# Two inner tiles of a feed-forward stage fed step by step at the start of a kernel, with a fixed order on TensorE and the inputs loaded first

## The chip, the cores and the metric

The kernel runs on one core of one Trainium2 chip. The metric is the device time of one execution, in microseconds. A profiled execution also has a span, from its first to its last instruction, which is a little shorter than its time.

## The reference

A two-layer backbone over 256 latent tokens x and 256 context tokens y, all of width 1024. Around each layer's token mixer (differential attention in layer 0, Fourier mixing in layer 1) stand two SwiGLU feed-forward stages, each behind an RMS norm and a shift and scale that are made from a condition vector:

```
m = silu(cond) @ w_mod + b_mod                    # per layer: 9 rows of 1024 (shift, scale, gate, three times)
h = rms_norm(x, norm_g) * (1 + scale) + shift
g, u = split(h @ w_gu)                            # D_FF = 2816
x = x + 0.5 * gate * ((silu(g) * u) @ w_d)
```

All is fp32, and the result must have fp32 accuracy. Latent tokens use the condition c, context tokens c_ctx. The change concerns only the start of the first of these stages in layer 0, on all 512 tokens.

## The kernel before, in words

The width of 1024 lies in 8 tiles of d with 128 rows each. xy holds both streams as d rows by 512 tokens. Accuracy comes from splitting each operand into a rounded part (hi) and the rest (lo); a product is then three matmuls, hi*hi, lo*hi, hi*lo (`mm3`, L140 to L143). `split` makes hi on ScalarE (L101) and lo on VectorE (L102), for weights in four pieces (`unit`, L130).

The start (L404 to L447) goes through the words of the table `START` (L31). A digit is `first_products` (L175): load a 1 MB chunk of w_mod (`raw_m`) and multiply it with the silu of both conditions, giving a row of shift and scale for one tile of d (`psr`, then `mrow` by a ScalarE copy). `x0` to `x3` load the inputs, two tiles of d each. `n` sums the squares, then `rstd_cols` (L248) adds them over the rows with products of one column (`ss`), GpSimd takes the power -1/2, four products against the identity spread it over all partitions (`rb`), and ScalarE copies it (`rstd`); VectorE and GpSimd then multiply x by it (`xr`, L443). `f` is `finish`: products of two columns turn the row of one tile of d into columns (`pst`, `first_columns`, L191), VectorE adds the constants (`amul`, `mod`), and shift and scale are applied to `xr` and split into `xop_hi` and `xop_lo`. `g0` and `g1` load and split the weights of the first two inner tiles; `c` loads the two conditions as rows over all partitions (`cond_x`, `cond_y`) and takes their silu (L205).

Then `gate_up` (L304) works through the 22 inner tiles of 128, all 512 tokens wide: for the gate part and the up part, the 8 tiles of d one after the other, 48 matmuls of 128x512 in all (`gu`), then silu on ScalarE (`sg`), a multiplication on VectorE (`hh`) and the split of h. The accumulators `psA` have two buffers, one inner tile each. Beside it VectorE makes the other shifts, scales and gates (`ada_steps`, L210): products of a w_mod chunk with a condition row (`junk`, L201).

All weight loads are issued by SyncE's queue in one order. A scheduler puts each engine's instructions in order by the costs that it assumes and by priorities (`high_priority`, with offsets 60 and 200); on the engines the order is then fixed. Weight tiles rotate in rings (`Ring`, L105), which have more buffers in some stages (`more_buffers`).

Of the kernel before, what the change touches and what calls it, by code (L numbers as in the profile page):

```python
# [14 lines left out]
P = 128  # L15
D = 1024
KT = D // P
NT = 256
# [57 lines left out]
def tile_kernel(ctx: ExitStack, tc, xyT, small, rows, tables, w_mod0, w_mod, w_gu, w_d0, w_d, w_qkv, w_o, w_f, out):  # L76
# [42 lines left out]
    @contextmanager  # L119
    def more_buffers(name, **counts):  # L120
        with ExitStack() as st:
            for tag, n in counts.items():
                pool = st.enter_context(tc.tile_pool(name=f"{name}_{tag}", bufs=n))
                rings[tag].extra = [pool] * n
                rings[tag].i = 0
            yield
            for tag in counts:
                rings[tag].extra = []

    def unit(ap, cols, name):  # L130
        with tc.high_priority(offset=AHEAD):
            raw = rings["raw"].tile(name)
            nc.sync.dma_start(raw[:, :cols], ap)
            hi, lo = rings["whi"].tile(name), rings["wlo"].tile(name)
            for i in range(PIECES):
                c = slice(i * cols // PIECES, (i + 1) * cols // PIECES)
                split(hi[:, c], lo[:, c], raw[:, c])
        return hi, lo

    def mm3(ps, sh, sl, mh, ml, start, stop):  # L140
        PE.matmul(ps, sh, mh, start=start, stop=False)  # L141
        PE.matmul(ps, sh, ml, start=False, stop=False)  # L142
        PE.matmul(ps, sl, mh, start=False, stop=stop)  # L143

    mhalf = const.tile([P, 8], F32, name="mhalf")
    V.memset(mhalf, -0.5)
# [28 lines left out]
    def first_products(dt, spool):  # L175

        raw = rings["raw"].tile(f"m0{dt}")
        nc.sync.dma_start(raw, w_mod0[dt])
        ps = pC(f"psr{dt}")

        for k in range(KT):
            q = k % 4 * 32
            PE.matmul(ps[q:q + 32, :256], cs[:, k, :], raw[:, k * 256:(k + 1) * 256], start=k < 4, stop=k >= 4)
# [7 lines left out]
    def first_columns(dt, row):  # L191
        pt = pB(f"pst{dt}")
        for m in (1, 0):
            PE.matmul(pt[:, 2 * m:2 * m + 2], row[:, m * P:(m + 1) * P], sel, start=True, stop=True)
        V.tensor_scalar(amul[:, 0, :, 0, dt], pt[:, 2:4], bm1[:, dt:dt + 1], sm[:, C_NG + dt:C_NG + dt + 1],
                        op0=ALU.add, op1=ALU.mult)
        V.tensor_scalar_add(mod[:, 0, :, 0, dt], pt[:, 0:2], sm[:, C_BM + dt:C_BM + dt + 1])
# [47 lines left out]
        else:  # L245
            eng.tensor_add(acc[:, sl], acc[:, sl], sq[:, sl])

    def rstd_cols(acc, sl, name):  # L248

        nt = (sl.stop - sl.start) // P  # L250
        ps = pB(f"ss_{name}")
        sq = tails.pop(sl.start)
        for t in range(nt):
            c = slice(sl.start + t * P, sl.start + (t + 1) * P)
            PE.matmul(ps[:, t:t + 1], acc[:, c], ones[:, 0:1], start=True, stop=False)
            PE.matmul(ps[:, t:t + 1], sq[:, c], ones[:, 0:1], start=False, stop=True)
# [6 lines left out]
    def finish_rstd(acc, sl, name, r=None):  # L263
        n = sl.stop - sl.start
        with tc.high_priority(offset=URGENT):
            rc = rstd_cols(acc, sl, name)
            ps = pB(f"rb_{name}")
            for t in range(n // P):
                PE.matmul(ps[:, t * P:(t + 1) * P], rc[:, t:t + 1].to_broadcast([P, P]), ident, start=True, stop=True)
            if r is None:  # L270
                r = work.tile([P, NT], F32, tag="rstd", name=f"rstd_{name}", bufs=2)
            S.copy(r, ps[:, :n])
        return r

    def new_acc(name):
# [7 lines left out]
    def modulated(layer, w, s, r, dt):  # L283
        sl = (SX, SY)[s]
        h = work.tile([P, 512], F32, tag="hh", name="hmod")
        sh = mod[:, layer, s, 3 * w, dt:dt + 1]
        V.scalar_tensor_tensor(h[:, :NT], xy[:, dt, sl], amul[:, layer, s, w, dt:dt + 1], r, op0=ALU.mult, op1=ALU.mult)
        S.activation(xop_hi[:, dt, sl], h[:, :NT], AF.Identity, bias=sh)
        V.scalar_tensor_tensor(xop_lo[:, dt, sl], h[:, :NT], sh, xop_hi[:, dt, sl].bitcast(F32),  # L289
                               op0=ALU.add, op1=ALU.subtract)  # L290


    def scaled_shift(layer, w):
# [7 lines left out]
                               op0=ALU.mult, op1=ALU.subtract)  # L301


    def gate_up(layer, f, j, n, rstd, h_hi, h_lo, jj, fpool):  # L304
        nn = n if rstd is None else NT + 2
        hi, lo = (layer == f == 0 and early.pop(j, None)) or unit(w_gu[layer, f, j], 2048, f"gu{layer}{f}{j}")
        ps = pA(f"gu_{layer}_{f}_{j}")
        for part in range(2):
            for k in range(KT):
                c = k * 256 + part * P  # L310
                mm3(ps[:, part, :nn], hi[:, c:c + P], lo[:, c:c + P], xop_hi[:, k, :nn], xop_lo[:, k, :nn],
                    k == 0, k == KT - 1)
# [12 lines left out]
        split(h_hi[:, jj, :], h_lo[:, jj, :], h[:, :n])  # L325
# [78 lines left out]


    acc = new_acc("l0f0")
    early = {}
    apool = tc.tile_pool(name="ada0", bufs=1)
    apool_ = apool.__enter__()
    conds = [cond_x, apool_.tile([P, D], F32, name="cond_y")]  # L410
    with tc.tile_pool(name="start", bufs=1) as spool, more_buffers("x0", **MORE0):
        def finish(dt):
            with tc.high_priority(offset=URGENT):
                first_columns(dt, begun[dt])
                h = work.tile([P, 512], F32, tag="hh", name="hmod")
                for s, sl in enumerate((SX, SY)):
                    a, sh = amul[:, 0, s, 0, dt:dt + 1], mod[:, 0, s, 0, dt:dt + 1]
                    if s == 0:
                        S.activation(h[:, sl], xr[:, dt, sl], AF.Identity, scale=a, bias=sh)
                    else:  # L420
                        V.tensor_scalar(h[:, sl], xr[:, dt, sl], a, sh, op0=ALU.mult, op1=ALU.add)
                split(xop_hi[:, dt], xop_lo[:, dt], h)

        xr = spool.tile([P, KT, 2 * NT], F32, name="xr")
        rstd0 = spool.tile([P, 2 * NT], F32, name="rstd0")

        pw = pA("warm")
        for _ in range(WARM):
            PE.matmul(pw[:, 0, :P], ones, ones, start=True, stop=True)
        begun = {}  # L430
        for what in START.split():
            if what == "c":
                for s in range(2):
                    condition(conds[s], s)
            elif what[0] == "x":
                i = 2 * int(what[1:])
                nc.sync.dma_start(xy[:, i:i + 2], xyT[:, i:i + 2])
            elif what == "n":
                for i in range(KT):
                    sumsq(acc, i, slice(0, 2 * NT), V)  # L440
                finish_rstd(acc, slice(0, 2 * NT), "l0f0", rstd0)
                for i in range(KT):
                    (V, G)[i in XR_G].tensor_mul(xr[:, i], xy[:, i], rstd0)  # L443
            elif what[0] == "g":
                early[int(what[1:])] = unit(w_gu[0, 0, int(what[1:])], 2048, f"gu00{what[1:]}")
            elif what[0] == "f":
                finish(int(what[1:]))  # L447
            else:
# [472 lines left out]
```

## Time and profile before

| | us |
|---|---|
| median of 3 runs | 1248.56 (1247.15 to 1249.66) |
| the profiled execution | 1248.28 |
| its span | 1246.5 |
| TensorE's products busy | 1219.0 (98%), 8540 instructions |
| TensorE's weight loads busy | 1124.2 (90%) |
| VectorE, ScalarE, GpSimd busy | 906.4, 553.8, 101.9 |

A matmul of full fp32 operands shows as two instructions in the trace and one in the listing of the order; a matmul on split operands is one in both. In the timeline a row is a run of equal instructions: its start, the time from its start to its end, the engine, line and tile, and in brackets the idle time ahead of it with what ended it. Matmuls overlap, so the distance between starts tells more than one's duration. PEclk is TensorE's granted clock: 1.00 is 2.4 GHz, 0.50 is 1.2 GHz.

### The profile page before, as it was taken

To read this page: it belongs to the slowest core of one execution; us is meant where nothing else is said; L and a number is where in the kernel's file an instruction comes from. 1 tells how busy PE (TensorE), PEld (TensorE's weight loads), DVE (VectorE), ACT (ScalarE), POOL (GpSimd) and SP (SyncE) were. 2 spreads that over 40 slices of the span, in tenths; PEclk is the share of its full clock that TensorE was granted. 3 is DMA by queue.
4 is the path that set the end of the run, shared out by engine and by line. 5 is a ranking of instruction groups with operands and counts; after the bars stand their busy time and mean duration, and the time that the engine had idled before them with its cause. 6 is when DMAs were issued, how large, how long until landed. Compare 5 with 4: busy or idle time off the path is not lost. (4 is left out here: it accounts for less than half of the span.)

```text
span 1246.5 us, 21265 instructions
## 1 busy us (share of the span) xinstructions
PE 1219.0 (98%) x8540; PEld 1124.2 (90%) x8540; DVE 906.4 (73%) x1756; ACT 553.8 (44%) x1215; POOL 101.9 (8%) x90
## 2 busy tenths in 40 slices
PE   6899999999999999999999999999999999999998
PEld 4688888888788989998899999999999999999998
DVE  2697985659883777787788787888688767666664
ACT  3432232223133445445545455555455545544552
POOL 1100000000001352340110000110000011000000
PEclk6799999999999899999999999999999999999999
DMA  9555474648881222121465676676686554536532
GB/s 367 212 210 195 171 253 147 215 147 315 302 349 52 84 102 102 61 77 67 156 224 203 246 300 224 210 293 235 206 307 243 176 195 181 181 126 246 188 117 81
DMA packets 37811, 241.94 MB, mean 194 GB/s; under 512 B 4224, under 2 KB 5376, under 8 KB 14672
## 3 DMA queue, kind: packets, MB, share of 16 engines
q1 hardware_dynamic: 37584, 240.25, 52.8%
q8 instruction: 67, 1.10, 0.3%
q0 software_dynamic: 128, 0.33, 0.2%
q14 instruction: 32, 0.26, 0.1%
HBM read 239.51 MB, written 1.05 MB: 193 GB/s over the span
## 5 line engine op out<-in xcount | busy, mean ns | idle before, releaser
L142 PE MATMUL gu<-xop_lo,whi_gu 128*128 128x258 f32 (+1 forms) x1408 | 441.2, 314 | 2.0 <-DVE xop_lo L300 1.5
L141 PE MATMUL gu<-xop_hi,whi_gu 128*128 128x258 f32 (+1 forms) x1408 | 440.7, 314 | 1.7 <-ACT whi_gu L101 1.4
L143 PE MATMUL gu<-xop_hi,wlo_gu 128*128 128x258 f32 (+1 forms) x1408 | 440.1, 313 | 0.1
L101 ACT CAST whi_gu<-raw_gu 128x512 fp32r<-128x512 f32 x352 | 194.8, 618 | 207.1 <-PE gu L142 120.8
L142 PEld LDWEIGHTS gu<-xop_lo,whi_gu 128*128 128x128 f32 x1408 | 268.5, 191 | 19.2 <-DVE xop_lo L300 2.0
L141 PEld LDWEIGHTS gu<-xop_hi,whi_gu 128*128 128x128 f32 x1408 | 268.7, 191 | 18.9 <-ACT whi_gu L101 1.7
L143 PEld LDWEIGHTS gu<-xop_hi,wlo_gu 128*128 128x128 f32 x1408 | 268.8, 191 | 16.7 <-DVE wlo_gu L102 0.4
L102 DVE TENSOR_TENSOR wlo_gu<-raw_gu,whi_gu 128x512 fp32r<-128x512 f32 x352 | 226.8, 691 | 64.6 <-ACT whi_gu L101 63.9
L142 PE MATMUL dn<-h_lo,whi_d 128*128 128x256 f32 (+1 forms) x724 | 219.6, 304 | 0.0
L143 PE MATMUL dn<-h_hi,wlo_d 128*128 128x256 f32 (+1 forms) x724 | 219.5, 304 | 0.0
L141 PE MATMUL dn<-h_hi,whi_d 128*128 128x256 f32 (+1 forms) x724 | 217.7, 304 | 0.4 <-DVE xy L339 0.4
L201 DVE SCALAR_TENSOR_TENSOR junk<-raw_m,cond_x 128x1024 f32<-128x1024 f32 x128 | 156.9, 1226 | 34.7 <-DMA raw_m<-in_w_mod 33.7
L101 ACT CAST whi_d<-raw_d 128x352 fp32r<-128x352 f32 (+2 forms) x256 | 105.9, 484 | 168.9 <-PE gu L142 87.8
L102 DVE TENSOR_TENSOR wlo_d<-raw_d,whi_d 128x352 fp32r<-128x352 f32 (+2 forms) x256 | 121.0, 526 | 54.9 <-ACT whi_d L101 54.9
L141 PEld LDWEIGHTS dn<-h_hi,whi_d 128*128 128x128 f32 x724 | 136.4, 189 | 7.0 <-PE dn L143 0.8
L142 PEld LDWEIGHTS dn<-h_lo,whi_d 128*128 128x128 f32 x724 | 136.8, 189 | 6.2
L143 PEld LDWEIGHTS dn<-h_hi,wlo_d 128*128 128x128 f32 x724 | 136.8, 189 | 6.0
L339 DVE SCALAR_TENSOR_TENSOR xy<-dn,mod,xy 128x256 f32<-128x256 f32 x112 | 50.5, 480 | 58.9 <-PE dn L143 58.7
L510 PE MATMUL pj<-whi_qkv,xop_hi 128*128 128x256 f32 x320 | 92.5, 289 | 0.7 <-DVE kr L556 0.7
L511 PE MATMUL pj<-wlo_qkv,xop_hi 128*128 128x256 f32 x320 | 91.7, 287 | 0.9 <-DVE wlo_qkv L102 0.9
L512 PE MATMUL pj<-whi_qkv,xop_lo 128*128 128x256 f32 x320 | 92.0, 289 | 0.2 <-DVE xop_lo L289 0.2
L101 ACT CAST h_hi<-hh 128x256 fp32r<-128x256 f32 (+1 forms) x88 | 40.3, 460 | 89.0 <-DVE hh L324 60.3
(224 smaller groups left out, 1406.4 us busy)
## 6 DMA issues: line engine op xcount, KB each, us to landing
raw_gu<-in_w_gu SPq DMA_DIRECT2D x88, 1024.0 KB, 5.1
raw_m<-in_w_mod SPq DMA_DIRECT2D x72, 1024.0 KB, 5.8
raw_d<-in_w_d SPq DMA_DIRECT2D x48, 704.0 KB, 4.1
raw_qkv<-in_w_qkv SPq DMA_DIRECT2D x12, 1024.0 KB, 4.8
raw_d<-in_w_d SPq DMA_DIRECT2D x8, 768.0 KB, 4.2
raw_d<-in_w_d SPq DMA_DIRECT2D x8, 640.0 KB, 4.8
raw_wo<-in_w_o SPq DMA_DIRECT2D x4, 1024.0 KB, 4.8
raw_wf<-in_w_f SPq DMA_DIRECT2D x4, 1024.0 KB, 7.2
```

Of the source, the lines that this page charges most:

```text
L101: S.copy(hi, src)
L102: V.tensor_sub(lo, src, hi.bitcast(F32))
L141: PE.matmul(ps, sh, mh, start=start, stop=False)
L142: PE.matmul(ps, sh, ml, start=False, stop=False)
L143: PE.matmul(ps, sl, mh, start=False, stop=stop)
L201: V.scalar_tensor_tensor(junk, w, 1.0, c, op0=ALU.mult, op1=ALU.mult, accum_out=out_col)
L339: V.scalar_tensor_tensor(xy[:, dt, so], ps[:, so.start - sl.start:so.stop - sl.start], mod[:, layer, s, 6 * f + 2, dt:dt + 1], xy[:, dt, s ...
L510: PE.matmul(ps[:, i], xh, wh, start=k == 0, stop=False)
L511: PE.matmul(ps[:, i], xh, wl, start=False, stop=False)
L512: PE.matmul(ps[:, i], xl, wh, start=False, stop=k == KT - 1)
```

## The change

The start is written as one longer table of words, and the products that it names are kept on TensorE in the order of the program (`keep`, a call that holds back the scheduler). The words: `x` loads two tiles of d of the inputs, `l` a chunk of w_mod, `G` and `H` the weights of the first and second inner tile; `p` multiplies a chunk of w_mod, `s` is squares and their sums, `r` spreads rstd, `t` makes the columns of one tile of d, `m` applies norm, shift and scale to one tile of d for both streams (`modulated`, the function that the attention stage already used), `g` and `h` split one piece of the first and second weight tile, behind the last ScalarE instruction of `r` or `m`. `a` and `b` are the six matmuls of one tile of d for the first and second inner tile, in two accumulators at once. `w` is three products of 128x256 whose result nobody reads. `c` loads the condition rows, now behind a one-column copy on GpSimd that reads the last tile's `amul`. `xr` and its multiplications are gone, the warming products are 20 and not 12, and the rings begin a stage with its added buffers.

```diff
-START = "0 x0 1 x1 2 x2 3 x3 n 4 g0 f0 5 f1 f2 6 f3 f4 7 g1 f5 c f6 f7"
-WARM = 12
+START = ("x0 x1 x2 x3 l0 l1 G l2 H l3 l4 l5 p0 s w p1 l6 l7 t0 w t1 w r g0 m0 m1 w g1 a0 p2 a1 h0 t2 m2 b0 p3 b1 h1 t3 m3 "
+         "a2 p4 b2 g2 t4 m4 a3 p5 b3 h2 t5 m5 a4 p6 b4 g3 t6 m6 a5 p7 b5 h3 t7 m7 a6 b6 a7 b7 c")
+WARM = 20
+IDLE = 3
...
-                rings[tag].i = 0
+                rings[tag].i = len(rings[tag].base)
...
+    def gate_up_part(ps, hi, lo, part, k, nn, hold=lambda i: i):
+        c = k * 256 + part * P
+        mm3(ps[:, part, :nn], hi[:, c:c + P], lo[:, c:c + P], xop_hi[:, k, :nn], xop_lo[:, k, :nn], k == 0, k == KT - 1,
+            hold)
...
-        hi, lo = (layer == f == 0 and early.pop(j, None)) or unit(w_gu[layer, f, j], 2048, f"gu{layer}{f}{j}")
-        ps = pA(f"gu_{layer}_{f}_{j}")
...
+        ps = (layer == f == 0 and begun.pop(j, None)) or None
+        if ps is None:
...
+            elif op in "gh":
+
+                with tc.issue_after(latest["S"]):
+                    j = "gh".index(op)
+                    if i == 0:
+                        first[j] = split_tiles(f"gu00{op}")
+                    split_piece(*first[j], raw[op], i, 2048)
...
+            elif op == "w":
+                pw = pB("idle")
+                for _ in range(IDLE):
+                    keep(PE.matmul(pw[:, :256], ones, xy[:, 0, :256], start=True, stop=True))
...
+            elif op == "m":
+                with tc.high_priority(offset=URGENT):
+                    for s in range(2):
+                        latest["S"] = modulated(0, 0, s, rstd0[:, s * NT:(s + 1) * NT], i).ins
+            elif op in "ab":
+                j = "ab".index(op)
+                if i == 0:
+                    begun[j] = pA(f"gu_0_0_{j}")
+                for part in range(2):
+                    gate_up_part(begun[j], *first[j], part, i, 2 * NT, keep)
+            else:
                 for s in range(2):
+
+                    G.tensor_copy(conds[s][:, :1], amul[:, 0, s, 0, KT - 1:])
                     condition(conds[s], s)
```

SyncE's queue at the program's start, before (xy is the inputs, raw_m a chunk of w_mod, raw_gu an inner tile's weights):

```order
L153 DMA sm<-in_small 128x209
L178 DMA raw_m_139<-in_w_mod 128x2048
L437 DMA xy<-in_xyT 128x1024
L178 DMA raw_m_153<-in_w_mod 128x2048
L437 DMA xy<-in_xyT 128x1024
L178 DMA raw_m_167<-in_w_mod 128x2048
```

The same place now:

```order
L168 DMA sm<-in_small 128x209
L443 DMA xy<-in_xyT 128x1024 x4
L135 DMA raw_m_150<-in_w_mod 128x2048
L135 DMA raw_m_152<-in_w_mod 128x2048
L135 DMA raw_gu00G<-in_w_gu 128x2048
L135 DMA raw_m_156<-in_w_mod 128x2048
```

All four input loads moved ahead of the first chunk of w_mod, and the first weights ahead of the third.

TensorE's products at the program's start, before (psr is a row of shift and scale, ss the column sums, rb the spread rstd, pst the columns):

```order
L429 MATMUL warm<-ones 128x128 x12
L183 MATMUL psr_141<-raw_m_139,cs 32x256 x8
L183 MATMUL psr_155<-raw_m_153,cs 32x256 x8
L183 MATMUL psr_169<-raw_m_167,cs 32x256 x8
L183 MATMUL psr_183<-raw_m_181,cs 32x256 x8
L255 MATMUL ss_l0f_216<-ones,ssacc_l0f_113 128x1
```

The same place now, up to the first gate/up product (idle is a group whose result nobody reads):

```order
L437 MATMUL warm<-ones 128x128 x20
L196 MATMUL psr_166<-raw_m_150,cs 32x256 x8
L268 MATMUL ss_l0f_198<-ones,ssacc_l0f_113 128x1
...
L460 MATMUL idle<-xy,ones 128x256 x3
L196 MATMUL psr_215<-raw_m_152,cs 32x256 x8
L207 MATMUL pst_230<-sel,mrow_175 128x2 x2
...
L207 MATMUL pst_239<-sel,mrow_224 128x2 x2
...
L280 MATMUL rb_l0f_248<-ident,rc_l0f_208 128x128 x4
...
L154 MATMUL gu_0_0_280<-xop_hi,whi_gu00g 128x512
```

The sums moved ahead of all w_mod products but the first, and six of the eight w_mod products moved behind the first gate/up product. Of the four idle groups one is shown; the others stand behind each pst group and behind rb.

ScalarE's queue where the second inner tile ends, before (sg is the silu of an accumulator, gu_0_0 the first inner tile, gu_0_1 the second; whi the rounded weights, 532 those of the third tile, 599 of the fourth):

```order
L101 CAST whi_gu_532<-raw_gu_530 128x512 x4
L316 ACTIVATE sg<-gu_0_0_420 128x512
L101 CAST whi_gu_599<-raw_gu_597 128x512 x4
L316 ACTIVATE sg<-gu_0_1_475 128x512
L101 CAST h_hi_418<-hh 128x512
```

The same place now (640 are the weights of the fourth tile, 573 of the third):

```order
L303 ACTIVATE xop_hi<-hmod,mod 128x256 x2
L221 ACTIVATE cond_x<-cond_x 128x1024
L104 CAST whi_gu_640<-raw_gu_638 128x512 x4
L337 ACTIVATE sg<-gu_0_0_280 128x512
L221 ACTIVATE cond_y<-cond_y 128x1024
L337 ACTIVATE sg<-gu_0_1_321 128x512
L104 CAST whi_gu_573<-raw_gu_571 128x512 x4
```

The third tile's casts moved from ahead of both silus to behind them, behind the silus of the conditions and behind the fourth tile's casts. On VectorE the corresponding pieces follow in the same order, with one `junk` product behind each condition and the multiplication `hh` of each tile behind its silu. On TensorE the second tile's last product is now followed by two products of the third tile, 19 of the fourth, and then the third tile's others.

## Rows read from the trace of the kernel before

**Rows 1.** Windows of the span: length, busy time (instructions), PEclk, DMA share, GB/s.

```profile
9.40:29.90 20.50, 13.99 (x99) 8.32 (x91) 6.25 (x11) 7.99 (x17) 1.03 (x1) 0.50 1.02 426
29.90:36.70 6.80, 3.34 (x43) 2.08 (x42) 6.80 (x7) 1.56 (x4) 6.29 (x4) 1.00 1.01 417
36.70:53.80 17.10, 15.38 (x56) 11.53 (x57) 11.22 (x33) 13.04 (x23) 0.01 (x1) 0.50 0.35 131
53.80:71.58 17.78, 17.78 (x77) 14.12 (x76) 10.91 (x19) 2.70 (x6) 0.00 (x0) 1.00 0.43 165
71.58:1246.50 1174.92, 1162.48 (x8237) 1082.54 (x8236) 870.42 (x1683) 527.05 (x1165) 92.80 (x77) 0.99 0.52 190
```

**Rows 2.** Timeline of TensorE's products up to 40 us.

```profile
1.09 5.26 PE L429 MATMUL warm<-ones 128*128 128x128 f32 x24 [1.09 <-DVE ones L160]
...
12.18 1.94 PE L183 MATMUL psr<-raw_m,cs 128*32 128x256 f32 x16 [2.22 <-DMA raw_m<-in_w_mod]
...
22.27 0.58 PE L255 MATMUL ss_l0f<-ones,ssacc_l0f 128*128 128x1 f32 x2 [0.66 <-DVE ssacc_l0f L246]
...
25.77 1.93 PE L183 MATMUL psr<-raw_m,cs 128*32 128x256 f32 x16
...
30.11 1.07 PE L183 MATMUL psr<-raw_m,cs 128*32 128x256 f32 x16
31.12 1.05 PE L194 MATMUL pst<-sel,mrow 128*128 128x2 f32 x8
...
37.95 1.87 PE L194 MATMUL pst<-sel,mrow 128*128 128x2 f32 x8 [4.48 <-DVE mod L197]
```

**Rows 3.** The same timeline: gate/up products at either clock, third tile's first.

```profile
46.26 0.63 PE L141 MATMUL gu<-xop_hi,whi_gu 128*128 128x512 f32 x1
46.69 0.63 PE L142 MATMUL gu<-xop_lo,whi_gu 128*128 128x512 f32 x1
...
56.89 0.39 PE L141 MATMUL gu<-xop_hi,whi_gu 128*128 128x512 f32 x1
57.12 0.40 PE L142 MATMUL gu<-xop_lo,whi_gu 128*128 128x512 f32 x1
...
71.58 0.50 PE L141 MATMUL gu<-xop_hi,whi_gu 128*128 128x512 f32 x1
```

**Rows 4.** DMA issues from 40 to 50 us: size, time to landing.

```profile
raw_gu<-in_w_gu SPq DMA_DIRECT2D x1, 1024.0 KB, 4.7
```

**Rows 5.** L287 and L288, `modulated` in the attention stage: ns min/median/max.

```profile
L287 DVE SCALAR_TENSOR_TENSOR hmod<-xy,amul,rstd_l0a x16: 478/485/486, 418.9 to 433.7; 128x256 f32<-128x256 f32 x16
L288 ACT ACTIVATE xop_hi<-hmod,mod x16: 493/508/512, 419.4 to 434.2; 128x256 fp32r<-128x256 f32 x16
```

**Rows 6.** Groups of ScalarE and GpSimd up to 40 us: busy us, mean ns.

```profile
L272 ACT COPY rstd<-rb_l0f 128x512 f32<-128x512 f32 x1 | 0.6, 585 | 0.2 <-PE rb_l0f L269 0.2
...
L149 POOL TENSOR_TENSOR rc_l0f<-nv_l0f,mhalf 128x4 f32<-128x4 f32 x1 | 1.0, 1032 | 23.5 <-DVE nv_l0f L259 23.5
...
L909 POOL MEMSET const-float32-0.0<- 128x1 f32 x1 | 0.1, 98 | 0.2 <-issue 0.2
```

**Rows 7.** Timelines of ScalarE (ACT) and VectorE (DVE), 43 to 72 us.

```profile
43.33 1.05 ACT L208 ACTIVATE cond_x<-cond_x 128x1024 f32<-128x1024 f32 x1
...
45.44 0.28 DVE L195 TENSOR_SCALAR amul<-pst,bm,sm 128x2 f32<-128x2 f32 x1 [2.12 <-PE pst L194]
...
48.27 2.17 ACT L101 CAST whi_gu<-raw_gu 128x512 fp32r<-128x512 f32 x4
...
52.48 1.89 DVE L102 TENSOR_TENSOR wlo_gu<-raw_gu,whi_gu 128x512 fp32r<-128x512 f32 x3
...
67.58 0.59 ACT L316 ACTIVATE sg<-gu 128x512 f32<-128x512 f32 x1
69.70 1.22 DVE L201 SCALAR_TENSOR_TENSOR junk<-raw_m,cond_x 128x1024 f32<-128x1024 f32 x1
...
70.85 0.68 DVE L317 TENSOR_TENSOR hh<-sg,gu 128x512 f32<-128x512 f32 x1
```

More of the change, by code (lines that the diff above doesn't have):

```diff
@@ L128, in more_buffers, with load, split_tiles, split_piece @@
                 rings[tag].extra = []
+    def load(ap, cols, name):
+        raw = rings["raw"].tile(name)
+        nc.sync.dma_start(raw[:, :cols], ap)
+        return raw
+    def split_tiles(name):
+        return rings["whi"].tile(name), rings["wlo"].tile(name)
+    def split_piece(hi, lo, raw, i, cols):
+        c = slice(i * cols // PIECES, (i + 1) * cols // PIECES)
+        split(hi[:, c], lo[:, c], raw[:, c])
     def unit(ap, cols, name):
         with tc.high_priority(offset=AHEAD):
[L132 to L134 removed]
+            raw = load(ap, cols, name)
+            hi, lo = split_tiles(name)
             for i in range(PIECES):
[L136 to L137 removed]
+                split_piece(hi, lo, raw, i, cols)
         return hi, lo
[L140 to L143, printed above, removed]
+    def mm3(ps, sh, sl, mh, ml, start, stop, keep=lambda i: i):
+        keep(PE.matmul(ps, sh, mh, start=start, stop=False))
+        keep(PE.matmul(ps, sh, ml, start=False, stop=False))
+        keep(PE.matmul(ps, sl, mh, start=False, stop=stop))
+    keep = tc.keep_in_program_order
     mhalf = const.tile([P, 8], F32, name="mhalf")
@@ L193, in first_columns @@
         for m in (1, 0):
-            PE.matmul(pt[:, 2 * m:2 * m + 2], row[:, m * P:(m + 1) * P], sel, start=True, stop=True)
+            keep(PE.matmul(pt[:, 2 * m:2 * m + 2], row[:, m * P:(m + 1) * P], sel, start=True, stop=True))
         V.tensor_scalar(amul[:, 0, :, 0, dt], pt[:, 2:4], bm1[:, dt:dt + 1], sm[:, C_NG + dt:C_NG + dt + 1],
@@ L246, in sumsq, with rstd_cols @@
             eng.tensor_add(acc[:, sl], acc[:, sl], sq[:, sl])
[L248 removed]
+    def rstd_cols(acc, sl, name, hold=lambda i: i):
         nt = (sl.stop - sl.start) // P
@@ L261, in rstd_cols, with spread_rstd, finish_rstd @@
         return rc
-    def finish_rstd(acc, sl, name, r=None):
-        n = sl.stop - sl.start
+    def spread_rstd(rc, n, name, r, hold=lambda i: i):
+        ps = pB(f"rb_{name}")
+        for t in range(n // P):
+            hold(PE.matmul(ps[:, t * P:(t + 1) * P], rc[:, t:t + 1].to_broadcast([P, P]), ident, start=True, stop=True))
+        return S.copy(r, ps[:, :n])
+    def finish_rstd(acc, sl, name):
         with tc.high_priority(offset=URGENT):
             rc = rstd_cols(acc, sl, name)
[L267 to L272, printed above, removed]
+            r = work.tile([P, NT], F32, tag="rstd", name=f"rstd_{name}", bufs=2)
+            spread_rstd(rc, sl.stop - sl.start, name, r)
         return r
@@ L301, in scaled @@
                                op0=ALU.mult, op1=ALU.subtract)
+    def gate_up_part(ps, hi, lo, part, k, nn, hold=lambda i: i):
+        c = k * 256 + part * P
+        mm3(ps[:, part, :nn], hi[:, c:c + P], lo[:, c:c + P], xop_hi[:, k, :nn], xop_lo[:, k, :nn], k == 0, k == KT - 1,
+            hold)
     def gate_up(layer, f, j, n, rstd, h_hi, h_lo, jj, fpool):
         nn = n if rstd is None else NT + 2
-        hi, lo = (layer == f == 0 and early.pop(j, None)) or unit(w_gu[layer, f, j], 2048, f"gu{layer}{f}{j}")
-        ps = pA(f"gu_{layer}_{f}_{j}")
[L308 to L312, printed above, removed]
+        ps = (layer == f == 0 and begun.pop(j, None)) or None
+        if ps is None:
+            hi, lo = unit(w_gu[layer, f, j], 2048, f"gu{layer}{f}{j}")
+            ps = pA(f"gu_{layer}_{f}_{j}")
+            for part in range(2):
+                for k in range(KT):
+                    gate_up_part(ps, hi, lo, part, k, nn)
         sg = work.tile([P, 512], F32, tag="sg", name="sg")
@@ L406, in tile_kernel @@
     acc = new_acc("l0f0")
-    early = {}
+    begun = {}
     apool = tc.tile_pool(name="ada0", bufs=1)
@@ L411, in tile_kernel @@
     with tc.tile_pool(name="start", bufs=1) as spool, more_buffers("x0", **MORE0):
[L412 to L424, printed above, removed]
         rstd0 = spool.tile([P, 2 * NT], F32, name="rstd0")
@@ L428, in tile_kernel @@
         for _ in range(WARM):
-            PE.matmul(pw[:, 0, :P], ones, ones, start=True, stop=True)
-        begun = {}
+            keep(PE.matmul(pw[:, 0, :P], ones, ones, start=True, stop=True))
+        raw, rows0, first, latest = {}, {}, {}, {}
+        everything = slice(0, 2 * NT)
         for what in START.split():
-            if what == "c":
+            op, i = what[0], int(what[1:] or 0)
+            if op == "x":
+                nc.sync.dma_start(xy[:, 2 * i:2 * i + 2], xyT[:, 2 * i:2 * i + 2])
+            elif op == "l":
+                raw[i] = load(w_mod0[i], 2048, f"m0{i}")
+            elif op in "GH":
+                raw[op.lower()] = load(w_gu[0, 0, "GH".index(op)], 2048, f"gu00{op}")
+            elif op in "gh":
[4 more added lines that the diff above has]
+                    split_piece(*first[j], raw[op], i, 2048)
+            elif op == "p":
+                rows0[i] = first_products(i, raw[i], spool)
+            elif op == "w":
+                pw = pB("idle")
+                for _ in range(IDLE):
+                    keep(PE.matmul(pw[:, :256], ones, xy[:, 0, :256], start=True, stop=True))
+            elif op == "s":
+                for k in range(KT):
+                    sumsq(acc, k, everything, V)
+                rc0 = rstd_cols(acc, everything, "l0f0", keep)
+            elif op == "r":
+                latest["S"] = spread_rstd(rc0, 2 * NT, "l0f0", rstd0, keep).ins
+            elif op == "t":
+                with tc.high_priority(offset=URGENT):
+                    first_columns(i, rows0[i])
+            elif op == "m":
+                with tc.high_priority(offset=URGENT):
+                    for s in range(2):
[4 more added lines that the diff above has]
+                    begun[j] = pA(f"gu_0_0_{j}")
+                for part in range(2):
+                    gate_up_part(begun[j], *first[j], part, i, 2 * NT, keep)
+            else:
```

29 lines of the change are left out of this document (6 added, 23 removed).

## The prediction

> **What bounds the kernel now.** I read the stretches by granted clock first, then TensorE's rows in order of time, then the queues of ScalarE and VectorE around the end of the second inner tile. TensorE bounds the program: from 71.58 us, where the third inner tile begins, to the end it is busy 1162.48 of 1174.92 us at a mean clock of 0.99 [rows 1]. The change leaves that work as it is, but for neighbours that a scheduler swapped. So the question is when the third tile's products run; today that is 71.58 us [rows 3].
>
> Before that TensorE loses time in two ways. It stands idle: 2.22 us for the second chunk of w_mod, 4.48 us at 37.95 for the scaled inputs [rows 2]. And it runs at 1.2 GHz: from 9.4 to 29.9 us, and again from 36.7 to 53.8 us, behind the idle time at 37.95 [rows 1, 2]. At 1.2 GHz a gate/up product starts every 0.43 us, at 2.4 GHz every 0.23 us [rows 3]. The first rise came at 29.9 us, 4.1 us after a stretch of wide products began at 25.77; the two-column and one-column products ahead of it (22.27 to 25.77) had not brought it [rows 1, 2].
>
> **The change part by part.**
>
> *Loads.* The four input loads go ahead of all weights. They take TensorE's first wait with them: the first chunk of w_mod now stands fifth. In the kernel before, the second chunk was there at 12.18 us [rows 2], with two chunks of 1.05 MB, one input load of 0.52 MB and the small table in the queue up to it; the first chunk now has four input loads, itself and the table, 0.52 MB more. At 426 GB/s [rows 1] that is 1.2 us: the first w_mod products start at 13.4 us. The 20 warming products (12 took 5.26 us [rows 2], so at most 8.8) end before 10 us: free, under that wait. The inputs are all there 2.5 us before that chunk, so the squares are done in time.
>
> *Up to the first gate/up product.* First w_mod products 1.94 us, column sums 3.5 us (22.27 to 25.77) [rows 2]: 18.8 us, against 25.77 before. Then stand, in this order, idle products, second w_mod products, columns of tile 0, idle, columns of tile 1, idle, spreading of rstd. An idle group is six passes of 256 columns. No row shows it; the warming products' 24 passes of 128 columns give 0.22 us each [rows 2], so twice that, 2.6 us at 1.2 GHz and 1.3 at 2.4. The ends are 1.4 us (six gate/up starts at the higher level [rows 3]) and 2.6. I let the clock rise as it did, 4.1 us after wide products begin: at 22.9 us, inside the second w_mod products. These end at 23.2; columns 0.53 (two took 1.05 [rows 2]), idle 1.3, columns 0.53, idle 1.3, spreading 8 passes of 0.11: 27.8 us. Now ScalarE copies rstd (0.59 us [rows 6]), casts the first weight piece (a quarter of 2.17 [rows 7]) and makes xop_hi of both streams (0.51 each [rows 5]): first gate/up product at 30.0. The second wants xop_lo: behind the copy VectorE has two hmod of 0.485, one weight piece (0.63, a third of 1.89) and two xop_lo, which I price as hmod [rows 5, 7], so 31.0. The idle group behind the spreading covers 1.3 of these 3.2 us. The multiplications of x by rstd on VectorE and GpSimd fall out.
>
> *The steps.* From 31.0 TensorE has 95 products of 0.233, six groups of w_mod products of 1.07 and six of columns of 0.53 [rows 2, 3]: 22.1 + 6.4 + 3.2 = 31.7 us. VectorE's share of one step is two hmod, two xop_lo, a weight piece and two small scalars, about 3 us of the step's 4.4; a chunk of w_mod takes 1.05 MB / 426 GB/s = 2.5 us. Both hide. The first two tiles are done at T = 62.7 us.
>
> *The hand-over.* Both tiles now end together. Before, the first tile's silu ran at 67.58 and its multiplication at 70.85, beside products of the second tile that went on to 71.58 [rows 3, 7]. The Trainium skill (Perfetto Trace Analysis, section Matmuls) asks for just that: independent groups of products should rotate through PSUM banks, so that emptying one overlaps the next group. Were that still so, the new order would hand over at T for nothing, and the sum would be 8.9 us faster. The row says otherwise for the new order, because of what now stands in the queues. The third tile's first product waits for a cast on ScalarE that stands behind: silu of cond_x, four casts for the fourth tile, silu of the first tile, silu of cond_y, silu of the second. The cond loads wait for a copy on GpSimd of a column that the last columns' products make, 24 products and one column group ahead of T, so at T-5.6. The copy of 128x1 lies between a fill of 128x1 (0.10 us) and an operation with arithmetic on 128x4 (1.03) [rows 6]; I take 0.1, the nearer, and 0.28 for the scalar ahead of it [rows 7]. With hand-overs between engines the loads leave at T-5.0. A lone 1.05 MB lands 4.7 us after issue [rows 4], half of that 1.2 us earlier: cond_x is there at T-1.5. ScalarE: silu 1.05 to T-0.5, casts 2.17 to T+1.7, silu 0.53, silu of cond_y 1.05, silu 0.53, first cast 0.55: T+4.4 [rows 7]. VectorE: the modulation product behind cond_x 1.22, four weight pieces behind the casts to T+3.2, multiplication 0.6, another 1.22, multiplication 0.6: T+5.7 [rows 7]. TensorE can issue two products of the third tile at T+4.4; then the first of the fourth tile waits for that multiplication, with all others queued behind it. Loss 5.7 - 0.5 = 5.2 us. The third tile's own load, issued at about T-4 behind the cond loads, lands near T+3 and is hidden by ScalarE's queue. Bounds: 0, if evacuation were all it cost, and 6.1, with the slow copy.
>
> *The clock behind that gap.* An idle time of 4.48 us was followed by 1.2 GHz [rows 1, 2], so this one is too, for about the 4.1 us that dense work took to bring it back: 2.05 us lost. Bounds: 0, and 8.5 if it lasts as long as from 36.7 to 53.8.
>
> *Sum.* 62.7 + 5.2 + 2.1 = 70.0 against 71.58: 1.6 us earlier. The profiled execution took 1248.28 us (span 1246.5 and 1.8 around it), 0.28 below the median of the runs: 1246.7 for a profile, 1247.0 as a median. A difference under 0.2%, 2.5 us, can't be told from no change.
>
> **The rivals.**
>
> *Faster: the hand-over costs less.* If the cond loads are early or VectorE clears the two tiles sooner, the third tile starts at about T+3.4, and the clock may hold: 66.1, 5.5 us ahead, 1243. With no loss at all it is 1239.7. For it: a sum of 11 queue entries can be too pessimistic, and a multiplication of 0.6 us is all that the accumulators themselves need. Against it: the queues are in order, and each entry has a measured price.
>
> *Slower: the clock comes up late.* Place: the columns' two-column products between the idle groups. From 40 to 53 us the engine was busy with gate/up, w_mod and columns in a mix, and stayed at 1.2 GHz [rows 1]. If idle and column groups in turn don't raise it, everything to the spreading runs at 1.2: 18.8 + 2.6 + 1.9 + 0.9 + 2.6 + 0.9 + 2.6 + 1.9 = 32.2 instead of 27.8, so 2.8 us later than now: 1251.4. If the steps too run at the lower level for 17.1 us, 8.5 on top of the forecast: 1255.5. It decides from about 4 us of added low clock. Against it: the first rise came under products of the same kind.
>
> *It doesn't do what it says.* The steps wait for w_mod, not for TensorE. That needs the transfers at little more than half of the 426 GB/s; each such step would then cost a microsecond or so, 1252 in all.
>
> **How the numbers follow.** Forecast 0.40 (own range 1246 to 1250), faster rival 0.38, late clock 0.20, transfers 0.02. The first is no change, the second faster, the last two slower: 0.38, 0.40, 0.22. The faster rival reaches to 1239.7 and the late clock to 1255.5; a tenth is left out on each side: 1241.5 to 1252.5.
>
> **What would show it.** Right: first w_mod products near 13.4 us; a granted clock of 1.0 ahead of the first gate/up product, that at 30; gate/up products 0.23 us apart up to about 63; then TensorE idle some 5 us, released by ScalarE's cast and VectorE's multiplication, and 0.5 in the clock behind it; dense work from 68 on. Wrong: no gap between second and third tile (faster), a clock of 0.5 at the first gate/up product (slower), waits for w_mod within the steps, or new idle time behind the fourth tile, which the swapped order there could bring and which I price at nothing because the rows after 71.58 hold only 12.4 us of idle time in all.

## The result, and the profile after

The changed kernel takes 1260.31 us (median of 4 runs, 1259.98 to 1261.45) against 1248.02 for the kernel before beside it (4 runs): a ratio of 1.0099, with a 95% interval of 1.0081 to 1.0116. It is 12.3 us slower, where 1.6 us faster was forecast. Its profiled execution took 1259.98 us, with a span of 1258.2.

The start went almost as forecast. TensorE's timeline of the changed kernel, from the first w_mod products to the third inner tile (the tiles `gu00g` and `gu00h` are the first two inner tiles, a bare `gu` a later one):

```profile
14.48 1.93 PE L196 MATMUL psr<-raw_m,cs 128*32 128x256 f32 x16 [7.20 <-DMA raw_m<-in_w_mod]
...
31.34 0.50 PE L154 MATMUL gu<-xop_hi,whi_gu00g 128*128 128x512 f32 x1 [0.84 <-ACT xop_hi L303]
32.19 0.50 PE L155 MATMUL gu<-xop_lo,whi_gu00g 128*128 128x512 f32 x1 [0.35 <-DVE xop_lo L304]
...
64.03 0.39 PE L156 MATMUL gu<-xop_hi,wlo_gu00h 128*128 128x512 f32 x1
68.88 0.67 PE L154 MATMUL gu<-xop_hi,whi_gu 128*128 128x512 f32 x1 [4.46 <-ACT whi_gu L104]
...
70.41 0.79 PE L154 MATMUL gu<-xop_hi,whi_gu 128*128 128x512 f32 x1 [0.43 <-DVE hh L338]
...
72.83 0.40 PE L154 MATMUL gu<-xop_hi,whi_gu 128*128 128x512 f32 x1
```

Both tiles are done at T = 64.4, the third starts at T+4.5, and the third product from there, the first of the fourth tile, waits for a multiplication, as in the forecast. The product at 72.83 is the ninth since 68.88; at 0.233 us each that is worth a dense start at 70.97, against 71.58 before [rows 3]: the new start is 0.6 us ahead.

So the loss lies behind it: the profiled executions are 11.7 us apart (1259.98 and 1248.28), which makes 12.3 us from there on. The stretches by granted clock, with the columns of [rows 1]:

```profile
11.00:24.70 13.70, 10.22 (x56) 6.76 (x56) 2.79 (x5) 2.76 (x6) 1.03 (x1) 0.50 1.01 427
24.70:69.10 44.40, 38.75 (x251) 27.94 (x252) 26.74 (x64) 20.29 (x42) 0.50 (x2) 1.00 0.56 216
69.10:72.50 3.40, 2.97 (x7) 1.87 (x7) 3.40 (x6) 2.33 (x5) 0.00 (x0) 0.51 0.72 294
72.50:1258.20 1185.70, 1161.75 (x8230) 1083.08 (x8229) 867.82 (x1686) 523.53 (x1158) 93.60 (x77) 0.99 0.53 188
```

In the last of them TensorE is busy for 1161.75 us, about as much as before, but idle for 23.95; in the stretch from the third tile to the end it was idle for 12.44 before [rows 1]. What TensorE waited for from 75 to 1242 us, in total, times and longest, before and after. Before:

```profile
PE gu L142 <- DVE xop_lo L300: 1.5, 2, 0.9
PE gu L141 <- ACT whi_gu L101: 1.4, 1, 1.4
...
```

After:

```profile
PE ss_l0f L268 <- POOL ssacc_l0f L259: 4.5, 1, 4.5
PE gu L154 <- DVE gus L343: 3.3, 2, 1.9
PE ss_l1f L269 <- ACT sq L255: 2.0, 1, 2.0
PE ss_l0a L269 <- ACT sq L255: 1.7, 1, 1.7
PE gu L154 <- DVE hh L338: 1.5, 1, 1.5
PE rb_l1f L280 <- POOL rc_l1f L164: 1.0, 1, 1.0
...
```

Six groups of waits, 1.0 to 4.5 us in all for each, that were not there, in stages that the diff does not seem to touch. The two rows of before are its longest; none of the six groups is over 0.4 us there. Their places, in the timeline of the changed kernel:

```profile
421.11 0.38 PE L269 MATMUL ss_l0a<-ones,sq 128*128 128x1 f32 x2 [1.71 <-ACT sq L255]
...
628.67 0.47 PE L268 MATMUL ss_l0f<-ones,ssacc_l0f 128*128 128x1 f32 x2 [4.48 <-POOL ssacc_l0f L259]
...
834.50 0.39 PE L154 MATMUL gu<-xop_hi,whi_gu 128*128 128x258 f32 x1 [1.93 <-DVE gus L343]
...
847.73 0.39 PE L154 MATMUL gu<-xop_hi,whi_gu 128*128 128x258 f32 x1 [1.35 <-DVE gus L343]
...
1061.04 0.38 PE L269 MATMUL ss_l1f<-ones,sq 128*128 128x1 f32 x2 [1.97 <-ACT sq L255]
...
1062.91 1.22 PE L280 MATMUL rb_l1f<-ident,rc_l1f 128*128 128x128 f32 x4 [1.04 <-POOL rc_l1f L164]
1063.78 0.56 PE L154 MATMUL gu<-xop_hi,whi_gu 128*128 128x258 f32 x1
```

At 628 and 1061 us a feed-forward stage opens its added buffers; the other places lie behind such a point. Take the last. At 1058 to 1063 us TensorE walks through the column sums and the spreading of rstd, each waiting for other engines, before the first gate/up product. In the kernel before, products of that stage's first tile stand ahead of these sums, and no wait is seen there:

```profile
1051.28 0.28 PE L141 MATMUL gu<-xop_hi,whi_gu 128*128 128x258 f32 x1
...
1053.80 0.28 PE L255 MATMUL ss_l1f<-ones,ssacc_l1f 128*128 128x1 f32 x2
```

Why the first tile's products could not stand there is in SyncE's loads of that stage, in their order, with what each waits for (DVE and PE are the semaphores of VectorE and TensorE, DMAHW those of earlier transfers). Before (11078 is the stage's first tile, 11291 its fourth):

```
L133 DMA raw_gu_11078<-in_w_gu 128x2048 [waits DMAHW4_49,DVE_49]
L133 DMA raw_gu_11149<-in_w_gu 128x2048 [waits DMAHW5_49,DMAHW0_49,DVE_49]
L133 DMA raw_gu_11220<-in_w_gu 128x2048 [waits DMAHW6_49,DVE_49]
L133 DMA raw_gu_11362<-in_w_gu 128x2048 [waits DMAHW7_49,DVE_49]
L133 DMA raw_gu_11291<-in_w_gu 128x2048 [waits PE_49]
```

After (11119 is the first tile, 11190 the second):

```
L135 DMA raw_gu_11190<-in_w_gu 128x2048 [waits DMAHW4_49,DVE_49]
L135 DMA raw_gu_11261<-in_w_gu 128x2048 [waits DMAHW5_49,DVE_49]
L135 DMA raw_gu_11332<-in_w_gu 128x2048 [waits DMAHW6_49,DMAHW1_49,DVE_49]
L135 DMA raw_gu_11474<-in_w_gu 128x2048 [waits DMAHW7_49,DVE_49]
L135 DMA raw_gu_11119<-in_w_gu 128x2048 [waits PE_49]
```

One load waits for TensorE alone: the one into the added buffer, which can only start once TensorE is through with what lay in that memory before. A ring hands out its buffers in turn, the old ones first and the added one last, and its counter says with which one a stage begins. With the counter at 0 the added buffer falls to the fourth tile, which is needed late. With the counter at the number of old buffers, the change's last small edit, it falls to the first tile, which is needed at once. (In each of the three later stages the ring of loads and the two rings of split weights get one buffer each, and the line moves all three; they were not tried one by one.) ScalarE's timeline shows the price: the first tile's cast stands third in the stage, and waits for its load. TensorE's last product ahead of the stage (`wf`) starts at 1057.89 us, the cast at 1063.07; loads of this size land 4.8 us after their issue here (median from 1032 to 1075 us), which fits.

```profile
1052.46 2.18 ACT L104 CAST whi_gu<-raw_gu 128x512 fp32r<-128x512 f32 x4 [0.32 <-PE wf L155]
...
1058.09 2.18 ACT L104 CAST whi_gu<-raw_gu 128x512 fp32r<-128x512 f32 x4 [0.32 <-PE wf L155]
...
1063.07 2.18 ACT L104 CAST whi_gu<-raw_gu 128x512 fp32r<-128x512 f32 x4 [2.08 <-DMA raw_gu<-in_w_gu]
```

```profile
1057.89 0.28 PE L156 MATMUL wf<-f_hi,wlo_wf 128*128 128x256 f32 x1
```

### The profile page after: what moved, and what is told of

Same layout as the page of the kernel before. It is cut to its first block, busy times and chain, and to the rows that moved or that the text cites. A ratio compares the mean times of both kernels' runs of the same rounds, so it can differ in the third digit from the quotient of the medians.

```text
span 1258.2 us, 21342 instructions
## 1 busy us (share of the span) xinstructions
PE 1219.9 (97%) x8580; PEld 1125.7 (89%) x8580; DVE 903.1 (72%) x1768; ACT 552.9 (44%) x1215; POOL 96.9 (8%) x88
## 5 line engine op out<-in xcount | busy, mean ns | idle before, releaser
L154 PE MATMUL gu<-xop_hi,whi_gu 128*128 128x258 f32 (+1 forms) x1376 | 427.9, 311 | 9.9 <-ACT whi_gu L104 4.5
L155 PE MATMUL gu<-xop_lo,whi_gu 128*128 128x258 f32 (+1 forms) x1376 | 427.7, 311 | 0.0
L156 PE MATMUL gu<-xop_hi,wlo_gu 128*128 128x258 f32 (+1 forms) x1376 | 426.8, 310 | 0.0
L154 PEld LDWEIGHTS gu<-xop_hi,whi_gu 128*128 128x128 f32 x1376 | 262.7, 191 | 26.6 <-ACT whi_gu L104 4.9
L104 ACT CAST whi_gu<-raw_gu 128x512 fp32r<-128x512 f32 x344 | 190.7, 618 | 209.9 <-PE gu L155 105.8
L155 PEld LDWEIGHTS gu<-xop_lo,whi_gu 128*128 128x128 f32 x1376 | 263.2, 191 | 14.7
L156 PEld LDWEIGHTS gu<-xop_hi,wlo_gu 128*128 128x128 f32 x1376 | 262.8, 191 | 14.7
L105 DVE TENSOR_TENSOR wlo_gu<-raw_gu,whi_gu 128x512 fp32r<-128x512 f32 x344 | 221.6, 689 | 61.3 <-ACT whi_gu L104 60.7
```

The costliest lines, as they stand in the source:

```text
L104: S.copy(hi, src)
L105: V.tensor_sub(lo, src, hi.bitcast(F32))
L154: keep(PE.matmul(ps, sh, mh, start=start, stop=False))
L155: keep(PE.matmul(ps, sh, ml, start=False, stop=False))
L156: keep(PE.matmul(ps, sl, mh, start=False, stop=stop))
```

## The experiments

Times are medians. The experiments ran on three chips (e1 to e4, e5 to e8, e9 to e12), each beside the kernel before, which took 1248.6 to 1249.0 us there; ratios are to it. "Counter" is where a ring begins when a stage adds buffers.

**e1: the counter back at 0.** The changed kernel with one line undone:

```
-                rings[tag].i = len(rings[tag].base)
+                rings[tag].i = 0
```

> The changed kernel, but a stage that opens more buffers sets the ring's counter to 0 again, as the kernel before does, so a stage's first tiles go to the old buffers. Theory C (the counter): the 11 us that the changed kernel loses behind the third tile come from the counter, which makes each stage's first tile take a buffer of the new pool, and the order of all engines follows from that. Then they go, idle time of TensorE behind the third tile is near the 12 us of the kernel before, and the third tile's weights are cast ahead of the cond vectors: its first product at about 66.4 us; 1243, between 1241 and 1247. Theory S (the start): the loss follows from the new start and its hand-over, which the later stages inherit as other arrival times; the counter changes little: 1256 or more.

1244.07 us (12 runs, 1242.02 to 1248.56), ratio 0.9973 [0.9959, 0.9987]. That is 16.2 us less than the changed kernel, and faster than the kernel before. The six groups are gone (none of them is over 0.2 us). What TensorE waits for longest from 75 to 1242 us is now what it was in the kernel before; the third row, five waits of 0.3 us, is new:

```profile
PE gu L155 <- DVE xop_lo L316: 1.6, 2, 0.9
PE gu L154 <- ACT whi_gu L104: 1.4, 1, 1.4
PE pj L547 <- DVE xop_lo L304: 1.3, 5, 0.3
```

Theory S, that the later stages inherit the new start, falls. (Executions of e1 lie up to 6.5 us apart, and the profiled one is among the long ones at 1248.36; its waits are read here, not its time. The last section comes back to this.)

**e2: the kernel before, with that line alone.**

```
-                rings[tag].i = 0
+                rings[tag].i = len(rings[tag].base)
```

> The kernel before with one line of the change: the ring's counter starts at the number of old buffers where a stage opens more. Theory C: the same stalls as in the changed kernel appear at about 95, 420, 630, 830 to 850 and 1060 us, 1257 to 1261 in all. Theory S: within 2 us of the kernel before, 1246 to 1250.

1257.47 us, 1.0074 [1.0061, 1.0087]: some 9 us for one line, without the new start. Waits came at 420, 628, 833 and 1056 to 1061 us; those at 95 us and behind 833 us, which the theory wanted too, did not.

**e3, e4, e5 and e10: the counter at the number of old buffers in one stage only.** For e3:

```
-                rings[tag].i = len(rings[tag].base)
+                rings[tag].i = len(rings[tag].base) if name == "x2" else 0
```

and likewise `"x4"` for e4, `"x1"` for e5, `"x0"` for e10.

> The changed kernel, with the counter at the number of old buffers only in the stage that opens before the second feed-forward block (from about 616 us on); 0 in the three others. Theory C: the loss of that stage alone, 4.9 us (lag of 2.1 us at 612 to 7.0 at 1010 between the traces): about 1248, 1246 to 1251. Theory S: 1256 or more.

> The changed kernel, with the counter at the number of old buffers only in the last stage (the last feed-forward block, from about 1050 us on); 0 in the three others. Theory C: the loss of that stage alone, 4.8 us (lag of 6.9 us at 1010 to 11.7 at 1065): about 1248, 1246 to 1250, with TensorE waiting for the squares' column sums ahead of that block's products. Theory S: 1256 or more.

> The changed kernel, with the counter at the number of old buffers only in the stage behind the first two tiles (third tile to the attention); 0 in the three others. Theory C: what is left of the changed kernel's loss against e1 once the losses of e3 (2.1 us) and e4 (5.2) are taken off its 16.2, so 8.9 us, of which 4.6 at the hand-over (third tile's dense start at 71.0 instead of 66.4 us) and 3 at 95 and 421 us: 1250 to 1254. If it is under 1248, the rest belongs to the buffers of the start itself.

> The changed kernel, with the counter at the number of old buffers only in the start; 0 in the three stages behind it. The losses of e5 (6.4 us), e3 (2.1) and e4 (5.2) against e1 sum to 13.7 of the changed kernel's 16.2 us. If they add up, 2.5 us are the start's: 1246.5. Against that, the only difference seen in the order is that the silu of cond_x stands ahead of the third tile's casts, which puts the third tile at 3.2 instead of 2.3 us behind the second: 1245.

| counter at the old buffers in | us | above e1 |
|---|---|---|
| no stage (e1) | 1244.07 | |
| the start (e10) | 1246.37 | 2.3 |
| behind the first two tiles (e5) | 1250.50 | 6.4 |
| second feed-forward stage on (e3) | 1246.18 | 2.1 |
| the last stage (e4) | 1249.26 | 5.2 |
| all four (the changed kernel) | 1260.31 | 16.2 |

The four sum to 16.0 of 16.2 us. Each ratio's interval is about 1.5 us to either side, so so close a sum is partly luck, but no stage is left out. e3 was to lose 4.9 us, a price read from the lag between two traces, and lost 2.1. Its trace has two of the new groups (4.5 and 2.2 us), but the two longest of e1's, 1.6 and 1.4 us, are gone: an order that brings new waits can take old ones away. In e4 the waits of the last stage come back alone:

```profile
1048.58 0.38 PE L268 MATMUL ss_l1f<-ones,ssacc_l1f 128*128 128x1 f32 x2 [0.52 <-POOL ssacc_l1f L259]
...
1050.92 0.38 PE L269 MATMUL ss_l1f<-ones,sq 128*128 128x1 f32 x2 [1.96 <-ACT sq L255]
...
1052.79 0.76 PE L280 MATMUL rb_l1f<-ident,rc_l1f 128*128 128x128 f32 x4 [1.04 <-POOL rc_l1f L164]
```

They are 3.5 us of e4's 5.2. Behind them the granted clock is at 0.50 from 1053.95 to 1056 us, so the stall costs more than its idle time.

In e10 the hand-over shows a loss: ScalarE's queue again has the silu of cond_x ahead of the third tile's casts, and that tile's first product waits 4.31 us instead of 2.26. e1, then e10:

```profile
68.67 0.50 PE L154 MATMUL gu<-xop_hi,whi_gu 128*128 128x512 f32 x1 [2.26 <-DVE hh L338]
```

```profile
62.77 1.06 ACT L221 ACTIVATE cond_x<-cond_x 128x1024 f32<-128x1024 f32 x1 [2.82 <-DMA cond_x<-in_rows]
63.73 2.16 ACT L104 CAST whi_gu<-raw_gu 128x512 fp32r<-128x512 f32 x4
...
68.16 0.80 PE L154 MATMUL gu<-xop_hi,whi_gu 128*128 128x512 f32 x1 [4.31 <-DVE hh L338]
```

**e6: the added buffer for the second tile.** Is it the lateness of the first tile, or does any other counter upset the order?

```
-                rings[tag].i = len(rings[tag].base)
+                rings[tag].i = len(rings[tag].base) - 1 if name == "x4" else 0
```

> As e4, but in the last stage the counter starts one lower, so the new buffers go to the second tile of the block instead of the first; 0 in the three other stages. Theory L (the first tile is late, because its load waits until the memory of the new buffer is free, and TensorE has nothing ahead of it): the second tile is needed one tile, some 5.8 us, later, so most of e4's 5.2 us goes: 1244 to 1246. Rival O (any counter other than 0 upsets the order of the scheduler): 1248 to 1250 as in e4.

1244.75 us, 0.7 above e1, which the intervals can't tell from nothing: 4.5 of e4's 5.2 us are gone. A cast still waits for the load into the added buffer, as late as in e4 (1053.67 us, there 1053.29), but a tile later is soon enough. Theory L holds.

```profile
1053.67 3.22 ACT L104 CAST whi_gu<-raw_gu 128x512 fp32r<-128x512 f32 x6 [2.17 <-DMA raw_gu<-in_w_gu]
```

**e7 and e8: what the start itself still loses.** In the changed kernel, as in e1, TensorE is idle for some 7 us ahead of the first w_mod products. Within that time the granted clock falls to 0.5, and it stays there until 24.7 us (the stretches above), in e1's profile until 28.9. e7 is e1 with

```
-WARM = 20
+WARM = 48
```

> As e1, with 48 warming products instead of 20, so that TensorE has no idle time of 6 to 7 us ahead of the first w_mod products (at 14.4 us) in which the granted clock falls to 0.5. Theory W (the low clock from 12 to 23 or 29 us paces the start): the first gate/up product at 26.4 us instead of 30.7 (32 to 33 where the clock came late), the third tile 4 to 6 us earlier: 1238, 1236 to 1240. Theory D (loads, squares and the queues of VectorE and ScalarE pace the start, and the clock little): 1242 to 1244.

1240.09 us, 0.9937 [0.9922, 0.9953]. Theory W holds. The warming products reach to the first w_mod products, and from there to the third tile the clock is 1.0; the first gate/up product comes at 26.64 us:

```profile
26.64 0.50 PE L154 MATMUL gu<-xop_hi,whi_gu00g 128*128 128x512 f32 x1 [0.84 <-ACT xop_hi L303]
```

```profile
6.70:62.00 55.30, 51.85 (x377) 39.28 (x375) 29.05 (x69) 22.41 (x47) 1.53 (x3) 1.00 0.73 299
```

e8 adds an idle group behind the second tile's last product:

```
-... a6 b6 a7 b7 c"
+... a6 b6 a7 b7 w c"
```

> As e7, with one more idle group (three products) on TensorE behind the second tile's last product, in the 2.3 us in which it waits for the third tile. Expected: the granted clock doesn't fall to 0.5 behind the hand-over, as it does for 3.4 us in e1 and e4, but not in e3, so 0 to 1.7 us less than e7; if the idle group holds up the third tile or the accumulators, up to 1 us more.

1240.33 us, no different from e7. There was nothing to win: in e7 the clock did not fall behind the hand-over's 2.26 us anyway.

**e9: the hand-over's order.** e7 with the third tile's casts behind the first tile's silu:

```
+            with tc.issue_after(latest["sg"]) if layer == f == 0 and j == 2 else nullcontext():
+                hi, lo = unit(w_gu[layer, f, j], 2048, f"gu{layer}{f}{j}")
...
+            latest["sg" if j == 0 else "x"] = S.activation(sg[:, :n], ps[:, 0, :n], AF.Silu).ins
```

> As e7, with the third tile's weight casts ordered behind the first tile's silu on ScalarE. In e7 the hand-over's 2.26 us of idle time are four casts (2.17 us), silu 0.59 and multiplication 0.68 in a row behind the first tile's last product, which ends 1.4 us ahead of the second's. Theory Q (ScalarE's queue order makes the gap): silu and multiplication come first, the third tile starts some 2 us earlier and the gap is under 0.5 us: 1238, 1237 to 1239. Theory A (the accumulators' or the weight buffers' release makes it, whatever the order): the gap stays at 2 us: 1240.

1238.11 us, 0.992 [0.9906, 0.9935]. Theory Q holds for the gap. ScalarE and TensorE in e7:

```profile
58.18 2.18 ACT L104 CAST whi_gu<-raw_gu 128x512 fp32r<-128x512 f32 x4 [2.36 <-issue]
60.27 0.59 ACT L337 ACTIVATE sg<-gu 128x512 f32<-128x512 f32 x1
...
59.34 0.39 PE L156 MATMUL gu<-xop_hi,wlo_gu00h 128*128 128x512 f32 x1
61.99 0.50 PE L154 MATMUL gu<-xop_hi,whi_gu 128*128 128x512 f32 x1 [2.26 <-DVE hh L338]
```

and in e9:

```profile
58.10 0.60 ACT L338 ACTIVATE sg<-gu 128x512 f32<-128x512 f32 x1 [2.54 <-PE gu L156]
58.60 4.25 ACT L104 CAST whi_gu<-raw_gu 128x512 fp32r<-128x512 f32 x8
...
59.08 0.39 PE L156 MATMUL gu<-xop_hi,wlo_gu00h 128*128 128x512 f32 x1
59.57 0.47 PE L154 MATMUL gu<-xop_hi,whi_gu 128*128 128x512 f32 x1
```

The silu that stood behind 2.18 us of casts now comes first, and 2.26 us of idle time on TensorE are gone. That is shown by the traces; the 2.0 us between the medians of e7 and e9 agree with it, but the two intervals overlap.

**e11 and e12: without the idle products.**

```
-IDLE = 3
+IDLE = 0
```

on e7 (e11) and on e1 (e12).

> As e7, without the products of the four idle groups (0 instead of 3 in each). Theory I (the idle products hold the clock): waits between narrow products are empty, the granted clock falls to 0.5 before or in the steps, and 3 to 8 us are lost: 1243 to 1248. Theory N (they only stand in the way): the spreading of rstd comes up to 4.4 us earlier, as far as w_mod's second chunk and the first gate/up weights are there, and the first gate/up product 1 to 3 us earlier: 1237 to 1239.

> As e1, without the products of the four idle groups, and with 20 warming products. Theory I: the granted clock rises only behind the first gate/up products, which then run at 0.43 us each for 4 us or more, and in some executions through the steps: 1246 to 1252. Theory N: at the lower clock the four idle groups take 2.9 us each, and the first two stand between the sums and the spreading; without them the spreading comes 3 to 5 us earlier, which pays for the lower clock: 1242 to 1244.

1237.13 us for e11, ratio 0.9918 [0.9906, 0.9930], 3.0 less than e7; and 1242.87 for e12, 0.9959 [0.9946, 0.9973], 1.2 less than e1. In both pairs the intervals overlap, so the idle products are shown to bring nothing, not to cost. Theory I was right about the clock and wrong about the time, which came out as theory N has it. In e11 the granted clock is at 0.5 from 18.4 to 28.7 us, and yet the first gate/up product comes 3 us earlier than in e7, at 23.68:

```profile
18.40:28.70 10.30, 8.11 (x37) 5.22 (x36) 6.06 (x15) 4.10 (x9) 0.03 (x1) 0.50 1.01 422
```

```profile
18.05 1.58 PE L207 MATMUL pst<-sel,mrow 128*128 128x2 f32 x8
19.48 2.05 PE L280 MATMUL rb_l0f<-ident,rc_l0f 128*128 128x128 f32 x8
23.68 0.80 PE L154 MATMUL gu<-xop_hi,whi_gu00g 128*128 128x512 f32 x1 [2.14 <-ACT xop_hi L303]
```

The low clock takes back 1.9 of these 3 us: at the third tile e11 is 1.1 us ahead (60.90 against 61.99). In these traces the idle products buy a clock at the price of standing in front of the work that they warm for, and the two come out about even. The Trainium skill (Perfetto Trace Analysis, section Matmul Optimizations) asks that matmuls run back to back, since the engine scales its power by utilization; by that rule e7 should beat e11. The runs don't show that where the matmuls that fill the time are idle ones on the path. e11 is the fastest kernel here, with e9 beside it: 10 us ahead of the kernel before by the ratio. The two edits together were not run.

## Why the prediction was wrong

*What failed* is the sentence under "What bounds the kernel now" that the change leaves the work from 71.58 us to the end as it is, but for neighbours that a scheduler swapped, and with it the price of nothing, because the rows there hold only 12.4 us of idle time. That idle time says how well the old order hid its waits, not what another order would. The one line on the ring's counter had no term in the sum and no rival, although it acts wherever a stage adds buffers; the description of the change lists it and yet says that only the start is concerned. It cost 16.2 us (e1), 13.7 of them in the stages that open behind the start (e5, e3, e4). In the profiles 12.3 us were lost behind the third tile's dense start, where the sum has nothing; of the line's 16.2 us that leaves some 4 for the hand-over, which the sum did price. New idle time behind the fourth tile stands among the signs of being wrong, so the risk was named, but no price was looked for. The slower rival, a late clock, was not the cause.

*Loads.* The first w_mod products came at 14.48 instead of 13.4 us; the rest of the start kept that delay. The 426 GB/s were not there early: up to 10 us 2.22 MB had moved, against 2.44 before, which is 0.5 us. The rest of it was not followed up.

*Up to the first gate/up product.* Clock up at 24.7 (forecast 22.9), first product at 31.34 (30.0), second at 32.19 (31.0): the steps hold, 1.2 to 1.8 us late, most of it from the first wait. An idle group took 2.91 us at the lower clock and 1.54 at the higher, forecast 2.6 and 1.3.

*The steps.* From 32.19 to T = 64.4 are 32.2 us, forecast 31.7; products 0.23 us apart, no wait for w_mod.

*The hand-over.* Third tile at T+4.5 (forecast T+4.4), the next wait ends at T+6.0 (T+5.7), from the very queue that was written down, and its entries are each within 0.4 us: silu of cond_x at T-1.1 (T-1.5), casts of the fourth tile to T+2.0 (T+1.7), first cast of the third at T+3.8 (T+3.8). That is not luck. ScalarE's queue as the cause is shown from both sides: with the silu of cond_x behind the casts the wait is 2.26 us (e1), with that silu put back 4.31 (e10), and with the first tile's silu ahead of the casts it is gone (e9). The queue was itself partly the counter's work. To ask what put cond_x first would have led to the line.

*The clock behind that gap.* 0.51 for 3.4 us, so 1.7 us at half speed; forecast 2.05.

*Sum.* A dense start at 70.97 instead of 70.0, 0.6 us ahead of before instead of 1.6. What was modelled was right to 1 us, in part by luck: T was 1.7 us late, and the hand-over with its clock took 6.6 us instead of 7.3. What was taken as unchanged lost 12.3.

*Left open.* Which entry of which queue makes each wait at 95, 421, 628, 834 and 848 us was not followed up. All go when the counter goes back to 0 (e1). The one at 421 us comes back in e5, the one at 628 and one of the two on `gus` in e3; the one at 95 us and the other on `gus` come back in no run with one stage alone, so more than one of them may be needed. How the counter does it is shown for the last stage alone (e4, e6).

*The faster rival* is near what the change does without its counter line: e1's third tile starts 2.3 us behind the second instead of 4.5, and e1 takes 1244.07, near the rival's 1243. But its reasons (early cond loads, a quicker VectorE) are not e1's, which has a shorter queue on ScalarE ahead of that tile.

## What to carry to other kernels

Before pricing the conspicuous part of a change, go through its small edits and ask of each where else it acts: a line in a helper that every stage calls needs a term for every stage. A buffer in memory that the stage before still uses should not go to the tile that is needed first; here one tile later gave back 4.5 of 5.2 us. In this kernel's load queue it is the load that waits for TensorE instead of for a buffer of its own ring. And the idle time of a stretch is a property of the present order, so "hardly idle today" is no bound on what a new order costs.

## What the hardware did that was not expected

In this start the granted clock does not rise at a fixed delay. e1 and e4 are the same up to 60 us in every instruction, and the first w_mod products start at 14.40 and 14.22 us. Still the granted clock came up at 28.9 us in the one profile and at 22.5 in the other (e1, then e4):

```profile
11.80:28.90 17.10, 14.50 (x69) 10.50 (x70) 2.46 (x7) 2.35 (x5) 1.03 (x1) 0.50 1.01 424
```

```profile
12.30:22.50 10.20, 8.28 (x42) 6.10 (x46) 1.43 (x3) 1.45 (x3) 1.03 (x1) 0.50 1.01 427
```

In five more profiles with the same order on TensorE up to there it came up at 22.5 (e6), 23.4 (e3), 23.6 (e10) and 24.7 us (e5 and the changed kernel). So the forecast's 4.1 us after wide products begin, read from one execution of the kernel before, is one draw of several. The executions of e1 show what it costs: seven took 1242.0 to 1244.1 us at a mean granted clock of 0.989 to 0.992, the other five 1247.4 to 1248.6 at 0.986 to 0.988. Where TensorE was kept busy with warming products up to the work (e7), the clock stayed at 1.0 until the third tile and beyond.

The fall differs as well. The same idle time of about 2.26 us at the hand-over was followed by 3.4 us at 0.5 in e1 and e4, and by none in e3 and e7.
